# A list-scheduled two-layer diffusion backbone: new costs for TensorE and GpSimd in the planner, and a larger threshold for holding an instruction back

## The chip, the core and the metric

One core of a Trainium2 chip runs the whole program. The metric is device time in microseconds (us), the median of the runs. The engines are called by the profile's names: PE (TensorE matmul), PEld (TensorE weight load), DVE (VectorE), ACT (ScalarE), POOL (GpSimd) and SP (SyncE, which issues the DMAs). Each engine runs its own instructions strictly in the order in which the program holds them and waits on semaphores for the others.

## What is computed

Two layers of a backbone act on 256 latent tokens and 256 context tokens of width 1024, all in float32:

```
for each layer:                                   # mod: shift, scale, gate from silu(c) @ ada_w
    x, ctx = half_ffn(x), half_ffn(ctx)           # h + 0.5*gate*(silu(h w1) * (h w3)) w2, width 2816
    y_x, y_c = mixer(modulate(rms_norm(x)), modulate(rms_norm(ctx)))
    x, ctx = x + gate*y_x, ctx + gate*y_c
    x, ctx = half_ffn(x), half_ffn(ctx)           # the last layer has no context from the mixer on
```

The even layer's mixer has grouped-query attention beside latent attention, with normed queries and keys and a rotary step, on one input and one output projection. The odd layer's has a gated linear recursion in both directions (HGRN2) beside neighbourhood attention.

## The kernel before, in words

**Tiles.** Activations lie transposed, 128 features on the partitions by up to 512 tokens. A weight of 128 x 1024 is loaded by SP, its high part is rounded to float32r on ACT (`_prep`, line 527), and the low part, the difference, comes from DVE or POOL (`tt("vp", ...)`, line 484). A projection is then three products per chunk (high x high, low x high, high x low; `mm3`), summed in one PSUM bank of 512 columns. Small products, such as attention's scores of the latent kind, its values, transposes and the recursion's levels, stay in plain float32.

**Stages.** `ffn` (line 761) runs four times: ffn, `ab` (line 1131), ffn, ffn, `cd` (line 1317), ffn. The last one has the 256 latent tokens alone. In `group` (line 891) one weight group meets tokens in blocks of 128, each block in the next of a ring of PSUM banks; the evacuation of such a bank norms the heads: a square on ACT, a sum on DVE, a reciprocal square root (`rsqrt`, line 488) of fourteen small dependent instructions on POOL, a product on DVE, then transposes on PE. In the even mixer the ring has five banks (0, 1, 2, 3, 6) and serves five groups in turn. In the odd mixer `hgrn` runs for each half of the heads: eight levels, each with a memset of a key buffer on POOL, copies into it on ACT, small products on PE, a masked copy on DVE, two multiplications on DVE and, for the next level, a product on POOL (512, 256, ... 8 elements wide).

**The order of the instructions** is written by no one. Every call is recorded as an operation with its dependences (`record`, line 203), and `schedule` (line 268) plays them through with costs in ns (`cost`, line 163), fixed latencies between engines (`LAT`, times 1.2) and, on all engines but tensor and sync, a margin of 1.02 on the cost. Buffers and banks are rings in the order of recording, so an operation also waits for the users of the buffer that it takes over. At each step the engine that is free first takes the most urgent of the operations that are ready. An operation recorded for two engines goes to the one that gets to it first, unless the other would end it earlier. Urgency comes from `latest` (line 337), a backward pass; `justified` (line 388) plays ten rounds and keeps the one whose planned end is the earliest. `issue` emits the operations in the order of their planned starts.

One rule may leave an engine idle. If an operation that is more urgent by GAP becomes ready within WAIT ns, and the one at hand is longer than LONG, the engine waits for the urgent one:

```
soon = min((q for q in lh if q[0] < t + self.WAIT and q[1] < p - self.GAP and q[3].start is None), ...)
if soon is not None and var[4] > self.LONG:
    c = (soon[0], soon[1], e, soon[3], soon[4])
```

The change touches `LONG` (line 144) and `cost` (line 163).

Of the kernel before, what the change touches and what calls it, by code (L numbers as in the profile page):

```python
# [126 lines left out]
def is_bytes(dt):  # L127
    return 1 if dt == U8 else 4
# [6 lines left out]
class Program:  # L135
# [5 lines left out]
        "gpsimd": dict(tensor=230, vector=75, scalar=100, gpsimd=100, sync=100),  # L141
        "sync": dict(tensor=200, vector=200, scalar=200, gpsimd=200, sync=0),
    }
    WAIT, GAP, LONG = 500, 150, 250

    MARGIN = 1.02
    LAT = {a: {b: t * 1.2 for b, t in d.items()} for a, d in LAT.items()}
# [15 lines left out]
    def cost(self, eng, name, a, k, out, ins):  # L163
        n = out.size if isinstance(out, View) else 0
        if eng == "tensor":
            m = 128 if name == "transpose" else a[1].size
            if name == "transpose":
                return 109
            if a[1].buf.dtype == F32R:
                return max(n / 2.4 + 2.5, 26 + 0.64 * m)  # L170
            tiles = 128 // (out.p1 - out.p0) if m <= 64 else 1
            return max(4 * max(n, m) / 2.4 / tiles + 5 * tiles, 80)
        if eng == "sync" or name == "dma_start":
            v = out if isinstance(out, View) else ins[0]
            return max(60, (v.p1 - v.p0) * v.size * is_bytes(v.buf.dtype) / 360)
        m = max([n] + [v.size for v in ins])
        src_ps = any(v.buf.psum for v in ins)
        ptrs = sum(isinstance(v, View) and v.size == 1 for v in list(a[2:]) + [k.get("scalar1"), k.get("scalar2")])
        if eng == "scalar":
            more = (k.get("accum_out") is not None) + any(isinstance(k.get(x), View) for x in ("bias", "scale"))  # L180
            return 0.833 * m + (51 if src_ps else 93) + 93 * more
        if eng == "gpsimd":
            if name == "memset":
                return 36 + 0.83 * n
            return 148 + (2.1 if name == "tensor_tensor" else 3.6 if ptrs else 0.85) * m
        fast = name in ("tensor_scalar", "tensor_copy", "memset") and not src_ps and not (isinstance(out, View) and out.buf.psum)
        return 69 + m * (0.53 if fast else 1.04) + (60 * ptrs if name in ("tensor_scalar", "scalar_tensor_tensor") else 0)

# [1533 lines left out]
```

## Time and profile before

| | |
|---|---|
| median of 3 runs | 1829.24 us (1828.5 to 1829.32) |
| the profiled execution | 1828.99 us |
| its span, first to last instruction | 1827.2 us |
| mean granted TensorE clock | 0.993 |
| PE busy | 1785.3 us, 98% of the span |
| DVE, ACT, POOL busy | 69%, 41%, 12% |

A busy time is the time in which at least one instruction of an engine ran. PE's instructions overlap, and the ends of its matmuls are modelled, so a row's mean duration of a matmul is longer than the distance from one to the next. Every recorded operation is emitted by one helper, so all rows bear line 408 and are told apart by engine, operation, tile and shape. The tile `b` is a PSUM bank; `wh` and `wl` are a weight's parts; `rq_v`, `rq_w` and `rq_i` belong to the reciprocal square root; `gH` and `gL` are reused, in the odd mixer for the recursion's operands.

### The profile page before, as it was taken

How to read it: one execution, taken by the hardware profiler on the slowest of the kernel's cores; microseconds unless marked ns; L12 is line 12 of the kernel's file. 1: busy time of each engine (PE TensorE's matmuls, PEld its weight loads, DVE VectorE, ACT ScalarE, POOL GpSimd, SP SyncE). 2: the span in 40 equal slices, each digit the busy share in tenths (PEclk: the TensorE clock that was granted, in tenths of full speed). 3: DMA queues.
4: the chain of work that ended last, by engine and by line, in shares of the span. 5: the costliest groups of instructions: out<-in, count | busy, mean ns of one | idle time of the engine just before them, and what ended most of it. 6: DMA issues, size and time to landing. Idle time of an engine off the chain costs nothing.

```text
span 1827.2 us, 25949 instructions
## 1 busy us (share of the span) xinstructions
PE 1785.3 (98%) x9795; PEld 1496.0 (82%) x9795; DVE 1256.6 (69%) x2251; ACT 742.4 (41%) x1270; POOL 224.9 (12%) x537
## 2 busy tenths in 40 slices
PE   7999999999899999999999999999999999989999
PEld 5888888898686798888888988888888877788887
DVE  5587777768778786666766765445458777777775
ACT  5422322236566452222222522222226548756553
POOL 0100000003442011000000100000004102511111
PEclk9999999999899999999999999999999999999999
DMA  8364555513011145444443454444433322146563
GB/s 348 119 204 171 201 189 175 173 50 113 27 47 58 58 130 171 160 163 160 161 156 109 142 173 162 161 147 175 156 121 105 118 84 72 43 153 196 186 195 104
DMA packets 75692, 257.59 MB, mean 141 GB/s; under 512 B 9392, under 2 KB 13232, under 8 KB 74288
## 3 DMA queue, kind: packets, MB, share of 16 engines
q1 hardware_dynamic: 75568, 255.94, 42.4%
q8 instruction: 77, 1.26, 0.3%
q14 instruction: 47, 0.39, 0.1%
HBM read 254.86 MB, written 1.05 MB: 140 GB/s over the span
## 4 chain that ended last, share of the span: by engine, by line
PE 90%; DVE 4%; POOL 3%; ACT 2%; issue 1%; DMA 0%; DVEq 0%; ACTq 0%; POOLq 0%
PE b L408 90%; POOL rq_w L408 1%; DVE w L408 1%; DVE wl L408 1%; POOL rq_v L408 1%; ACT gL L408 1%; DVE m L408 0%; POOL rq_i L408 0%; DVE gH L408 0%; ACT w L408 0%; POOL gH L408 0%; DVE nacc L408 0%; DMA xX<-in_xT 0%; DVE p L408 0%; DVE ss L408 0%
## 5 line engine op out<-in xcount | busy, mean ns | idle before, releaser
L408 PE MATMUL b<-hH,wh 128*128 128x512 f32 (+1 forms) x1648 | 600.1, 382 | 3.4 <-DVE hH L408 2.9
L408 ACT CAST wh<-raw 128x1024 fp32r<-128x1024 f32 (+4 forms) x310 | 312.2, 1008 | 638.4 <-PE b L408 506.6
L408 PE MATMUL b<-hH,wl 128*128 128x512 f32 (+1 forms) x1616 | 560.6, 356 | 0.4 <-DVE wl L408 0.4
L408 DVE TENSOR_TENSOR wl<-raw,wh 128x1024 fp32r<-128x1024 f32 (+4 forms) x309 | 384.5, 1247 | 162.9 <-ACT wh L408 159.8
L408 PEld LDWEIGHTS b<-hH,wh 128*128 128x128 f32 x1648 | 307.2, 189 | 61.1 <-DVE hH L408 3.2
L408 PEld LDWEIGHTS b<-hH,wl 128*128 128x128 f32 x1616 | 305.1, 189 | 50.1 <-issue 2.5
L408 PE MATMUL b<-hL,wh 128*128 128x512 f32 (+1 forms) x1232 | 294.2, 374 | 0.0
L408 DVE SCALAR_TENSOR_TENSOR adas<-ada,m 128x1024 f32<-128x1024 f32 x224 | 273.4, 1221 | 26.5 <-DMA ada<-in_adaT 24.0
L408 PE MATMUL b<-gH,wh 128*128 128x512 f32 (+1 forms) x809 | 278.8, 366 | 0.0
L408 PE MATMUL b<-gH,wl 128*128 128x512 f32 (+1 forms) x809 | 263.9, 341 | 0.0
L408 PEld LDWEIGHTS b<-hL,wh 128*128 128x128 f32 x1232 | 219.4, 188 | 42.3 <-issue 1.6
L408 PEld LDWEIGHTS b<-gH,wh 128*128 128x128 f32 x809 | 150.7, 188 | 24.1
L408 PEld LDWEIGHTS b<-gH,wl 128*128 128x128 f32 x809 | 151.9, 188 | 21.5
L408 DVE SCALAR_TENSOR_TENSOR xX<-b,mod,xX 128x256 f32<-128x256 f32 x152 | 72.6, 482 | 100.3 <-PE b L408 98.6
L408 PE MATMUL b<-gL,wh 128*128 128x512 f32 (+1 forms) x633 | 135.2, 354 | 0.0
L408 PEld LDWEIGHTS b<-gL,wh 128*128 128x128 f32 x633 | 106.5, 188 | 17.5
L408 ACT ACTIVATE w<-b 128x512 f32<-128x512 f32 (+3 forms) x104 | 58.7, 566 | 152.5 <-PE b L408 152.3
L408 DVE TENSOR_TENSOR w<-w,b 128x512 f32<-128x512 f32 x66 | 45.4, 687 | 96.1 <-PE b L408 95.8
L408 PE MATMUL b<-wh,hH 128*128 128x512 f32 (+3 forms) x288 | 105.1, 368 | 2.9 <-ACT hH L408 1.7
L408 PE MATMUL b<-wl,hH 128*128 128x512 f32 (+3 forms) x288 | 105.0, 366 | 0.0
L408 PE MATMUL b<-wh,hL 128*128 128x512 f32 (+3 forms) x288 | 104.2, 364 | 0.0
L408 POOL TENSOR_TENSOR gL<-w,gH 128x512 fp32r<-128x512 f32 x22 | 31.5, 1432 | 584.4 <-ACT gH L408 584.4
(216 smaller groups left out, 1924.9 us busy)
## 6 DMA issues: line engine op xcount, KB each, us to landing
raw<-in_w SPq DMA_DIRECT2D x182, 512.0 KB, 3.5
ada<-in_adaT SPq DMA_DIRECT2D x128, 512.0 KB, 4.4
raw<-in_w SPq DMA_DIRECT2D x56, 448.0 KB, 3.4
ada<-in_w SPq DMA_DIRECT2D x22, 512.0 KB, 3.6
gH<-in_ada SPq DMA_DIRECT2D x4, 1024.0 KB, 10.2
raw<-in_ab_out SPq DMA_DIRECT2D x8, 512.0 KB, 3.7
raw<-in_cd_z SPq DMA_DIRECT2D x8, 512.0 KB, 3.6
ada<-in_w SPq DMA_DIRECT2D x8, 448.0 KB, 3.3
```

The lines of the kernel that those rows point to most:

```text
L408: getattr(getattr(nc, e), name)(*[fix(v) for v in a], **{n: fix(v) for n, v in k.items()})
```

## The change

`LONG` goes from 250 to 500. In `cost`, the formulas for PE, for POOL's instructions other than memset, and for DVE's scan are replaced. No instruction is added or removed and none gets other operands; the planner reckons anew, so the order on each engine, and the engine of the operations that have a choice, may differ. No other constant of the planner changes.

```diff
-    WAIT, GAP, LONG = 500, 150, 250
+    WAIT, GAP, LONG = 500, 150, 500
...
         if eng == "tensor":
-            m = 128 if name == "transpose" else a[1].size
             if name == "transpose":
-                return 109
+                return 110
             if a[1].buf.dtype == F32R:
-                return max(n / 2.4 + 2.5, 26 + 0.64 * m)
-            tiles = 128 // (out.p1 - out.p0) if m <= 64 else 1
-            return max(4 * max(n, m) / 2.4 / tiles + 5 * tiles, 80)
+                return max(n / 2.4 + 14, 110)
+            if a[1].size <= 64:
+                return max((0.98 if out.p1 - out.p0 == 64 else 0.6) * n, 79)
+            return max(4 * n / 2.4 + 10, 222)
...
         if eng == "gpsimd":
             if name == "memset":
                 return 36 + 0.83 * n
-            return 148 + (2.1 if name == "tensor_tensor" else 3.6 if ptrs else 0.85) * m
+            return (220 + 3.2 * min(m, 256) + 2.1 * max(m - 256, 0)) if name == "tensor_tensor" else 235 + (3.6 if ptrs else 0.9) * m
+        if name == "tensor_tensor_scan":
+            return 70 + 2.07 * m
         fast = name in ("tensor_scalar", "tensor_copy", "memset") and not src_ps and not (isinstance(out, View) and out.buf.psum)
         return 69 + m * (0.53 if fast else 1.04) + (60 * ptrs if name in ("tensor_scalar", "scalar_tensor_tensor") else 0)
```

Here `n` is the number of elements per partition that are written, `m` the largest such number among the operands, and `ptrs` the number of operands that are one column.

## Rows read from the trace of the kernel before

**Rows 1.** The page, part 1: busy us, share of the span, instructions.

```profile
PE 1785.3 (98%) x9795; PEld 1496.0 (82%) x9795; DVE 1256.6 (69%) x2251; ACT 742.4 (41%) x1270; POOL 224.9 (12%) x537
```

**Rows 2.** Windows by stage: length, PE, PEld, DVE, ACT, POOL busy, PEclk, DMA, GB/s.

```profile
25.30:407.00 381.70, 381.68 (x1880) 315.73 (x1881) 274.32 (x441) 114.79 (x167) 23.20 (x30) 1.00 0.51 169
407.00:645.00 238.00, 225.63 (x1332) 181.33 (x1330) 186.15 (x523) 141.59 (x345) 69.00 (x260) 0.98 0.19 60
645.00:1372.00 727.00, 726.98 (x3602) 615.14 (x3601) 449.38 (x689) 212.01 (x295) 34.28 (x28) 1.00 0.46 154
1372.00:1637.20 265.20, 251.66 (x1861) 212.09 (x1859) 203.68 (x367) 165.63 (x279) 71.17 (x193) 0.98 0.31 97
1637.20:1823.30 186.10, 185.98 (x1056) 162.32 (x1056) 128.69 (x188) 94.94 (x158) 27.00 (x22) 0.99 0.54 169
```

**Rows 3.** The same view in finer windows of the two mixers.

```profile
456.90:463.30 6.40, 0.22 (x1) 0.01 (x1) 3.76 (x6) 0.90 (x2) 5.92 (x31) 0.67 0.22 61
463.30:469.40 6.10, 6.08 (x19) 5.05 (x20) 4.58 (x7) 3.21 (x5) 4.04 (x20) 0.51 0.01 3
...
1575.30:1579.60 4.30, 0.27 (x4) 0.05 (x2) 0.64 (x2) 1.85 (x3) 3.11 (x3) 0.89 0.46 149
1579.60:1585.60 6.00, 6.00 (x50) 4.71 (x52) 4.82 (x9) 4.84 (x8) 0.95 (x1) 0.51 0.06 25
1585.60:1630.00 44.40, 44.23 (x468) 42.33 (x464) 33.24 (x55) 27.67 (x46) 11.84 (x33) 1.00 0.38 121
1630.00:1637.20 7.20, 2.18 (x12) 1.83 (x12) 6.68 (x20) 4.16 (x8) 0.00 (x0) 0.73 0.61 209
1637.20:1640.20 3.00, 2.98 (x10) 2.69 (x11) 3.00 (x8) 1.93 (x5) 0.74 (x1) 0.52 0.51 175
```

**Rows 4.** Timelines of PE, DVE and POOL around 457: start, us, instruction [idle before].

```profile
463.32 1.09 PE L408 MATMUL b<-ident,w 128*128 128x128 f32 x4 [6.20 <-DVE w L408]
...
454.05 0.69 DVE L408 TENSOR_REDUCE ss<-w 128x8 f32<-128x512 f32 x1
...
454.82 0.20 POOL L408 TENSOR_SCALAR rq_v<-ss 128x8 f32<-128x8 f32 x1 [5.13 <-DVE ss L408]
...
462.25 0.20 POOL L408 TENSOR_TENSOR ss<-rq_i,rq_w 128x8 f32<-128x8 f32 x1
```

**Rows 5.** Timelines from 1568 to 1580, POOL and PE.

```profile
1568.40 6.45 POOL L408 TENSOR_TENSOR gH<-gH 128x512 f32<-128x512 f32 x7
...
1574.82 1.82 POOL L408 TENSOR_TENSOR wl<-raw,wh 128x768 fp32r<-128x768 f32 x1
1576.58 1.84 POOL L408 MEMSET gL<- 128x1024 f32 x2
...
1579.58 1.71 PE L408 MATMUL b<-gL 128*64 128x32 f32 x28 [4.03 <-ACT gL L408]
```

**Rows 6.** One window of the first feed-forward block, columns as in rows 2.

```profile
100.00:200.00 100.00, 100.00 (x438) 81.82 (x437) 76.96 (x113) 24.63 (x29) 4.26 (x3) 1.00 0.56 188
```

**Rows 7.** Groups of POOL by shape: count | busy us, mean ns | idle before.

```profile
L408 POOL TENSOR_TENSOR gL<-w,gH 128x512 fp32r<-128x512 f32 x22 | 31.5, 1432 | 584.4 <-ACT gH L408 584.4
L408 POOL TENSOR_TENSOR gH<-w,gH 128x256 fp32r<-128x256 f32 x20 | 25.5, 1276 | 140.1 <-ACT gH L408 140.1
L408 POOL TENSOR_TENSOR hL<-w,hH 128x256 fp32r<-128x256 f32 x20 | 15.9, 796 | 162.3 <-ACT w L408 162.3
...
L408 POOL TENSOR_TENSOR rq_w<-rq_v,rq_i 128x8 f32<-128x8 f32 x42 | 10.1, 244 | 2.7
```

**Rows 8.** A group of DVE in the page's part 5.

```profile
L408 DVE SCALAR_TENSOR_TENSOR xX<-b,mod,xX 128x256 f32<-128x256 f32 x152 | 72.6, 482 | 100.3 <-PE b L408 98.6
```

**Rows 9.** Timelines of POOL and DVE at 1562.

```profile
1561.75 1.96 POOL L408 TENSOR_TENSOR rq_w<-rq_v,rq_i 128x4 f32<-128x4 f32 x1
...
1562.45 1.19 DVE L408 TENSOR_TENSOR wl<-raw,wh 128x1024 fp32r<-128x1024 f32 x1
```

## The prediction

> **What bounds the kernel now.** First the busy shares of the page [rows 1]: PE is busy 98% of the span, and no other engine comes over 69%. Then the busy time by stage [rows 2]. In the three stretches of feed-forward work PE is busy 381.68 of 381.70 us, 726.98 of 727.00 and 185.98 of 186.10: nothing that only reorders instructions can shorten them unless it removes PE work, and this change removes none. The reader is to see that all slack sits elsewhere: PE idles 238.00 - 225.63 = 12.4 us in the even layer's mixer (407 to 645) and 265.20 - 251.66 = 13.5 us in the odd layer's mixer (1372 to 1637.2). The first 25.3 us and the last 3.9 us hold the other idle time: loading and a last residual, whose costs the change does not touch.
>
> Then the same view, cut finer around the long waits [rows 3]. Three holes carry most of the mixers' idle time: 6.40 us with 0.22 us of PE work at 456.9, 4.30 us with 0.27 at 1575.3, and 7.20 us with 2.18 at 1630. After each of them the granted clock is about one half, that is 1.2 of 2.4 GHz, for 6.10, 6.00 and 3.00 us, though PE is then busy. At half clock half of that time is lost: 3.05, 3.0 and 1.5 us. So the three holes cost 6.2 + 3.05, 4.0 + 3.0 and 5.0 + 1.5 us. What is left of the mixers' 25.9 us of idle time is 25.9 - 15.2 = 10.7 us, in many short waits.
>
> Last the timeline at the two first holes. At 463.32 PE resumes with a transpose after 6.20 us of waiting for a product on DVE [rows 4]. That product waits for a reciprocal square root on POOL, which began at 454.82, right after DVE's reduction at 454.05, and whose last instruction starts at 462.25 [rows 4]: 7.4 us for fourteen small instructions, because other such chains share POOL. At 1579.58 PE starts a level of the HGRN recursion that waited for ScalarE, which waited for two memsets on POOL at 1576.58. In front of these POOL had seven products, 6.45 us from 1568.40, and a weight's low part of 1.82 us that could as well have run on DVE [rows 5].
>
> **PE's new costs.** One float32r product of 512 columns goes from 215.8 to 227.3 ns in the plan. In a full stretch the trace has 438 records in 100.00 us, 228 ns each [rows 6]: the new figure is right, the old one 5% short. PE does the same work at the same pace, so this is worth nothing directly. What it moves is the plan's idea of how far PE has got when a chain on POOL or DVE ends.
>
> **POOL's new costs.** With the margin of 1.02, a product or subtraction of 512 elements goes from 1247 to 1609 ns, of 256 from 700 to 1060, of 16 from 185 to 276, of 8 from 168 to 250. The trace's means are 1432 for the 512-wide subtraction, 1276 and 796 for two kinds of 256, 244 for 8 [rows 7]: nearer to the new figures than to the old, one of the 256-wide kinds excepted. For the hole at 1575 the seven products of one half (512, 256, 128, 64, 32, 16 and 8 wide) were planned at 1247 + 700 + 425 + 288 + 219 + 185 + 168 = 3.2 us. They took 6.45 us [rows 5]. The new plan gives them 1609 + 1060 + 643 + 434 + 329 + 276 + 250 = 4.6 us. So the old plan believed POOL free 3.2 us too early, and thought that the weight's low part fitted before the memset. The new plan is still 1.9 us short, but that low part of 768 now costs 2157 ns on POOL and stays at 885 on DVE, so it should go to DVE, or behind the memset. That frees the 1.82 us. Bounds for this hole: nothing, to the whole 4.0 us. I take 2.2, just over the one instruction that stands there by mistake, and 1.0 of the 3.0 us of slow clock, since the trace has the half clock behind the longest waits alone. A loss here is not excluded; it is priced below.
>
> For the hole at 457 the product waits for chains that the old plan put at 166 ns an instruction and the new one at 250. Fourteen in a row, each with the plan's 120 ns of latency, are 4.0 us by the old figures and 5.2 by the new; the trace has 7.4. The new plan is nearer and starts the chain's sources, the reduction on DVE among them, earlier in the order. But what could fill PE meanwhile is limited: the products of the next groups use the same five banks in turn, and these are held until the chains end. I take 2.2 us of the 6.2, the step from 5.2 to 7.4 being what the plan still doesn't see, and 1.5 of the 3.05 us of slow clock. Bounds: nothing, to 9.2 us together.
>
> **Which engine takes the optional work.** An instruction that may run on DVE or POOL is moved to POOL when DVE would end it later. For the 512-wide low part this needs a DVE delay of over 1247 - 613 = 634 ns before, over 1609 - 613 = 996 after. So POOL loses some of its 22 such subtractions [rows 7], and DVE gains at most 22 x 0.61 = 13.5 us. This hides under PE: DVE is busy 274.32 of 381.70 us in the first feed-forward stretch and less than that share in the second [rows 2]. If that cover went, it would be those 13.5 us at most. I take nothing.
>
> **The scan** on DVE is planned at 612 instead of 342 ns: sixteen instructions, no work changed; nothing.
>
> **Holding back.** LONG goes from 250 to 500 ns. Instructions planned between the two no longer leave the engine idle for a more urgent one that comes within 500 ns. The residual of 256 columns is one, planned at 403 ns and 482 in the trace [rows 8]. Such an instruction can now delay an urgent one by its own length, while the engine loses less idle time. Bounds: a gain inside the 10.7 us of short waits, or a loss that the rivals price. Of the short waits I take 1.0 us off for plan and threshold together, with 4 us either way, since a new order moves these waits as easily as it ends them. The hole at 1630 is the last norm before a feed-forward block: nothing else is left for PE there, so it stays.
>
> **Sum.** 2.2 + 1.0 + 2.2 + 1.5 + 1.0 = 7.9 us. The profiled execution took 1828.99 us (span 1827.2), 0.25 us under the median of 1829.24, so one sum serves both: 1829.0 - 7.9 = 1821.1 us, call it 1821.
>
> **Rivals.** *No change: POOL's time is set by its neighbour.* At 1561.75 one 4-wide product on POOL takes 1.96 us, where an 8-wide one takes 0.20 [rows 4], and DVE's two-operand subtraction that starts at 1562.45 and takes 1.19 us ends at 1563.64, as the POOL instruction ends [rows 9]. If the long POOL times come from what DVE happens to run beside them, a fixed cost places no wait better, and the holes only move: about 1829, within 3.6 us. Beside it stands the Trainium skill, page "SBUF — State Buffer", section "Who interferes with whom": a VectorE instruction with two SBUF inputs contends with a GpSimd instruction that reads SBUF, and the later one waits for the whole of the other. By that rule no constant describes POOL; the trace agrees at this one place. For the rival also speaks that five shared banks limit what can fill the first hole; against it, that the mean of a group already has such waits in it. Chance 0.23.
>
> *Slower: short work in front of the odd layer's chain.* In the second half of the recursion the chain runs from POOL over ScalarE to PE and DVE and back, eight times, while the out-projection's eight residuals and as many squares for the norm run on DVE and ScalarE. All of these are short in the plan, so none is held back any more. If each stands in front of a chain instruction for the 0.482 us of a residual [rows 8], the chain ends 16 x 0.482 = 7.7 us later, and PE has nothing else once the out-projection is through: 1829 + 7.7 = 1836.7. It decides if these delays exceed what the two holes give back, that is from about 8 of the 16 on, if the holes give half of their 6.9 us. For it: the old threshold kept exactly these apart. Against it: between 1585.6 and 1630 PE is busy 44.23 of 44.40 us [rows 3], so some delay is covered. Chance 0.21.
>
> *Full gain.* Both holes close and the clock stays up: 9.2 + 7.0 us, and 1 of short waits: 1829 - 17 = 1812. Chance 0.08.
>
> *The change doesn't do what it says*: PE's and POOL's costs are means only of some kinds (796 against 1276 for one width [rows 7]), so the plan may be no truer than before. Its time is that of the first rival, and its chance is within that one's.
>
> **How the numbers follow.** The forecast, 1814 to 1825, has 0.48; with the full gain, faster is 0.56. A change under 0.2% of 1829, some 3.7 us, is about what a measurement of this kernel cannot tell from none: 0.23, and slower 0.21. The range goes from 1810, within the full gain, to 1835, within the slower case; what it leaves out is a few hundredths below and about 0.14 above. The likeliest case's own range is 1814 to 1825.
>
> **What would show it.** In the changed kernel: the feed-forward stretches as long as before within a microsecond; fewer than 22 of the 512-wide subtractions on POOL; no weight's low part on POOL in front of a memset in the recursion; PE's wait for the first rsqrt chains shorter than 6.2 us; less time at half clock. The forecast is wrong if the mixers' two stretches together are not shorter than 503.2 us (238.0 + 265.2), if new holes of several microseconds stand elsewhere in them, or if DVE now holds PE up in the feed-forward work.

## The result, and the profile after

| | before | after |
|---|---|---|
| median of 4 runs each, us | 1829.28 (1828.5 to 1830.81) | 1842.56 (1838.09 to 1844.42) |
| ratio, with its 95% interval | | 1.0069 [1.0056, 1.0082] |
| profiled execution, us | 1828.99 | 1838.09 |
| its span; mean granted clock | 1827.2; 0.993 | 1836.3; 0.996 |

The change makes the kernel 13.3 us slower. The forecast was 8 us faster, 1821 us; 1842.56 lies above its range of 1810 to 1835. The execution that was profiled is the fastest of the four.

The page of the kernel after, part 1 (busy us, share, instructions), answers to [rows 1]:

```profile
PE 1799.2 (98%) x9795; PEld 1494.0 (81%) x9795; DVE 1257.4 (68%) x2300; ACT 744.7 (41%) x1276; POOL 152.3 (8%) x482
```

PE runs the same 9795 instructions, has a higher mean clock, and is busy 13.9 us longer than before. The reader is to see that first: PE's work is the same, and it needs more time for it.

Windows of the kernel after, columns as in [rows 2]: the first and the second feed-forward stretch, one window within the first (as [rows 6]), the first long wait of the even mixer with what follows it and a second wait, the place of the hole at 1575, and the last norm.

```profile
21.90:411.30 389.40, 389.38 (x1894) 317.76 (x1895) 274.30 (x455) 115.83 (x169) 10.35 (x20) 1.00 0.50 170
654.56:1381.40 726.84, 726.63 (x3519) 605.16 (x3520) 438.01 (x683) 202.41 (x277) 7.71 (x8) 1.00 0.45 152
...
100.00:200.00 100.00, 100.00 (x431) 80.73 (x430) 76.25 (x116) 24.12 (x28) 0.00 (x0) 1.00 0.53 182
...
461.50:466.05 4.55, 0.39 (x3) 0.04 (x1) 3.05 (x5) 0.00 (x1) 4.22 (x22) 0.96 0.25 81
466.00:470.00 4.00, 3.88 (x14) 3.07 (x14) 2.15 (x4) 2.32 (x4) 2.58 (x16) 0.61 0.05 21
480.90:484.07 3.17, 0.41 (x3) 0.01 (x1) 1.84 (x6) 2.65 (x4) 2.59 (x14) 1.00 0.00 0
1575.00:1620.00 45.00, 42.06 (x479) 36.85 (x478) 35.25 (x52) 37.13 (x62) 12.40 (x23) 1.00 0.31 98
1639.00:1644.30 5.30, 1.51 (x7) 1.16 (x7) 3.65 (x18) 1.18 (x3) 0.00 (x0) 0.58 0.57 189
1644.30:1649.50 5.20, 5.18 (x17) 4.50 (x18) 4.57 (x11) 4.29 (x9) 1.47 (x2) 0.50 0.00 0
```

In the mixers the planner did much of what was hoped. The first hole is down from 6.40 to 4.55 us, and behind it stand 4.00 us at a clock of 0.61 where 6.10 us at 0.51 stood before [rows 3]; a hole of 3.17 us follows at 480.9, with the clock at 1.00. Around 1575 the clock is 1.00 throughout. But in the window from 100 to 200, where PE is busy all the time at full clock in both kernels, 438 records [rows 6] have become 431. The windows of whole stretches do not hold the same products before and after (3602 records in 727.00 us [rows 2], 3519 in 726.84), so their lengths do not compare; the same products are followed further down.

What PE waited for, in total, times, longest (us). The three lines of the kernel before:

```profile
PE b L408 <- DVE w L408: 9.2, 5, 6.2
PE b L408 <- ACT gL L408: 4.6, 2, 4.0
...
PE b L408 <- ACT p L408: 0.8, 1, 0.8
```

and of the kernel after:

```profile
PE b L411 <- DVE w L411: 4.9, 3, 4.2
PE b L411 <- ACT p L411: 2.8, 1, 2.8
PE b L411 <- DVE nrs L411: 2.4, 2, 2.1
...
PE b L411 <- ACT gL L411: 1.9, 4, 0.6
```

The two forecast waits shrank, 6.2 to 4.2 us and 4.0 to 0.6; the new one at 481 is the 2.8 us for a softmax tile `p`. So the 13.3 us are not in PE's waits. They are in the distance from one product to the next. The timeline of PE, four successive records before (start, us, instruction):

```profile
221.15 0.39 PE L408 MATMUL b<-hH,wh 128*128 128x512 f32 x1
221.38 0.39 PE L408 MATMUL b<-hH,wl 128*128 128x512 f32 x1
221.60 0.39 PE L408 MATMUL b<-hH,wh 128*128 128x512 f32 x1
221.83 0.39 PE L408 MATMUL b<-hH,wl 128*128 128x512 f32 x1
```

and after:

```profile
219.75 0.40 PE L411 MATMUL b<-hH,wl 128*128 128x512 f32 x1
219.99 0.40 PE L411 MATMUL b<-hH,wh 128*128 128x512 f32 x1
220.22 0.40 PE L411 MATMUL b<-hH,wl 128*128 128x512 f32 x1
220.46 0.40 PE L411 MATMUL b<-hH,wh 128*128 128x512 f32 x1
```

The same two products in turn: 0.68 us for three steps before, 0.71 after. It is the same instruction on tiles of the same shape at the same granted clock. What differs is where the tiles lie. A tile gets its address at its first use in the issued order (`make`, called by `issue`), so a new order gives new addresses. In the compiled programs (each tile's start in bytes within its partition) one 32-byte slot (`nrs`, buffer 1) lies in front of `mod0`, `gL` and `hH` before and behind them after, so that `gL` and `hH` start 32 bytes lower, at 320 instead of 352 bytes past a multiple of 512; `hL` and ten of the twelve weight buffers start at 352 in both. `gH` starts at 0 in both.

### The profile page after: what moved, and what is told of

Read it like the earlier page. It is cut to its first block, busy times and chain, and to the rows that moved or that the text cites. A ratio compares the mean times of both kernels' runs of the same rounds, so it can differ in the third digit from the quotient of the medians.

```text
span 1836.3 us, 25848 instructions
## 1 busy us (share of the span) xinstructions
PE 1799.2 (98%) x9795; PEld 1494.0 (81%) x9795; DVE 1257.4 (68%) x2300; ACT 744.7 (41%) x1276; POOL 152.3 (8%) x482
## 4 chain that ended last, share of the span: by engine, by line
PE 90%; DVE 4%; ACT 4%; issue 1%; POOL 1%; DMA 0%; ACTq 0%; DVEq 0%
PE b L411 90%; ACT gL L411 2%; DVE w L411 1%; DVE wl L411 1%; ACT wh L411 1%; DVE hL L411 0%; ACT w L411 0%; DVE gH L411 0%; DVE m L411 0%; DMA xX<-in_xT 0%; POOL rq_w L411 0%; ACT L411 0%; ACT gH L411 0%; DVE nacc L411 0%; ACT m L411 0%
## 5 line engine op out<-in xcount | busy, mean ns | idle before, releaser
L411 DVE TENSOR_TENSOR wl<-raw,wh 128x1024 fp32r<-128x1024 f32 (+4 forms) x310 | 363.7, 1174 | 227.3 <-ACT wh L411 223.5
L411 POOL TENSOR_TENSOR nacc<-nacc,w 128x256 f32<-128x256 f32 x5 | 7.3, 1457 | 735.4 <-ACT w L411 731.4
```

The source lines that it names most:

```text
L411: getattr(getattr(nc, e), name)(*[fix(v) for v in a], **{n: fix(v) for n, v in k.items()})
```

## The experiments

**Theory (places):** PE's pace depends on where the moving tile and the weights lie, and the new addresses cost the time. **Rival (order):** the new order itself slows PE, by what runs beside it. To tell them apart, a kernel's first buffers are made in a fixed order, whatever the instructions' order is. This edit is in every experiment; they differ in the list `LAYOUT`, and in whose planner they have:

```diff
     def issue(self, nc):
         end, order = self.justified()
+        sb = self.rings["ones"][0].pool
+        for tag, n in LAYOUT:
+            if tag == "pad":
+                sb.tile([128, 8], F32, tag=f"pad_{n}", name=f"pad_{n}")
+            else:
+                self.rings[tag][n].make()
```

A pad takes 32 bytes. Each kernel ran beside the kernel before on the same chip, and its ratio is against that.

**1. The changed planner with the old places.** The list has the first uses of the kernel before.

```diff
+    ("nrs", 0), ("pt", 0), ("vA", 0), ("nrs", 1), ("mod0", 0), ("gL", 0), ("hH", 0), ("hL", 0),
```

> The changed kernel's order of instructions, but every tile and bank at the address that it has in the kernel before. Places theory (the new order hands out other addresses, since a tile gets its place at its first use, and the distance between PE's products depends on them): the window from 100 to 200 us has about 438 products again instead of 431, the first feed-forward stretch is back from 389 to about 382 us, and the time falls by 12 to 22 us below the changed kernel's, to between 1820 and 1830. Order theory (the instructions that now run beside PE slow it): 431 products stay, and the time stays within 4 us of the changed kernel's.

Measured: 1826.26 us (11 runs) against 1828.88, ratio 0.9987 [0.9979, 0.9996]. The change's order, without its addresses, is 2.6 us faster than before. The stretch named in the expectation did not come back to 382 us: by windows set in the same way it is 387.90, with 1897 records. Those bounds take in other work than before; over the same products the sign holds, as the table behind experiment 12 shows (288.0 us from the first to the second column, 287.8 before, 292.0 after).

**2. The old planner with the new places.** The list has the first uses of the kernel after.

```diff
+    ("vA", 0), ("pt", 0), ("mod0", 0), ("gL", 0), ("hH", 0), ("nrs", 1), ("hL", 0),
```

> The kernel before in its own order, with every tile and bank at the address that it has in the changed kernel. Places theory: about 431 products in the window from 100 to 200 us, and 1840 to 1850 us in all. Order theory: 438 products and 1829 us, as before.

Measured: 1844.44 us (5 runs), ratio 1.0085 [1.0072, 1.0099]. The addresses alone cost 15.6 us. The window from 100 to 200 in experiment 1:

```profile
100.00:200.00 100.00, 100.00 (x437) 81.86 (x436) 76.57 (x116) 24.17 (x28) 0.00 (x0) 1.00 0.54 186
```

and in experiment 2:

```profile
100.00:200.00 100.00, 100.00 (x431) 80.74 (x430) 76.20 (x110) 24.72 (x29) 4.26 (x3) 1.00 0.56 185
```

The pace follows the places (437 and 431), not the order: the rival falls. DVE's and POOL's load in experiment 2 (76.20, 4.26) is near that of the kernel before (76.96, 4.26 [rows 6]), so what runs beside PE is not the cause either. Since the kernel after and experiment 1 have the same order, their 9795 records pair one to one. The kernel after gains 3.9 us of lag on experiment 1 from 100 to 390, nothing (0.1) from 390 to 645, 9.0 from 645 to 1372, and 1.3 from there to 1740: it loses where large products stand back to back.

**3. All tiles 32 bytes higher.** The old planner and places, with one pad in front.

```diff
-    ("ones", 0), ("xX", 0), ("pt", 2),
+    ("pad", 0), ("ones", 0), ("xX", 0), ("pt", 2),
```

> The kernel before with one unused piece of 32 bytes in front of all tiles: every tile moves by 32 bytes, and the distances between tiles stay. Absolute form of the places theory (a moving operand that starts at an odd multiple of 32 bytes streams at about 227 ns a product of 512 columns, one at a multiple of 64 at about 233): hH, hL and gL change to 64, gH to odd, so the distances swap, 431 to 433 products in the window, and 1838 to 1845 us. Relative form (what counts is whether weight and moving operand lie alike): nothing changes, 438 products, 1829 us. Order theory: nothing changes.

Measured: 1828.71 us (10 runs), ratio 0.9998 [0.9989, 1.0007]. No absolute address matters; only places relative to each other do.

**4. `gH` moved by 32 bytes, all behind it by 64.** A first form of the theory held that moving tile and weights must agree modulo 64.

```diff
-    ("gH", 0), ("nacc", 1),
+    ("pad", 0), ("gH", 0), ("pad", 1), ("nacc", 1),
```

> The kernel before with gH, alone of the four moving operands at a multiple of 64 bytes, moved to an odd multiple of 32; all other tiles keep their address modulo 64. Both forms of the places theory: products with gH go from about 233 to 227 ns; there are some 1000 of 512 columns, so 5 to 7 us less than before, 1822 to 1824 us. Order theory: 1829 us, no change.

Measured: 1828.55 us (10 runs), ratio 0.9995 [0.9986, 1.0004]. A miss. `gH` now starts at 32 past a multiple of 512 and the weights at 416: they agree modulo 64 and 128 but not modulo 256 or 512, and the products of `gH` are no faster on the whole. The next form was modulo 512.

**5 and 6. All weights and activations at the same place modulo 512.** `gH` moves behind `hL`, and the two odd weight buffers behind the other ten; all start at 352. Experiment 5 has the old planner, 6 the changed one.

```diff
-    ("gH", 0), ("nacc", 1), ("adab1", 0), ("rq_v", 0), ("rq_i", 0), ("wh", 0), ("rq_w", 0), ("wl", 0),
+    ("nacc", 1), ("adab1", 0), ("rq_v", 0), ("rq_i", 0), ("rq_w", 0),
...
-    ("hL", 0), ("wh", 1),
+    ("hL", 0), ("gH", 0), ("wh", 1),
...
-    ("wh", 5), ("wl", 5), ("ada", 0),
+    ("wh", 5), ("wl", 5), ("wh", 0), ("wl", 0), ("ada", 0),
```

> The kernel before in its own order, with gH, wh's first and wl's first buffer laid among the other large tiles, so that all moving operands and all weight buffers of the feed-forward blocks start at 352 modulo 512. Places theory in the form that the trace now suggests (a product is fast when its moving operand and the weight loaded beside it start at the same address modulo 512): some 1000 products with gH and a sixth of the others lose 5 to 6 ns, 8 to 12 us in all: 1817 to 1821 us, 440 records in the window. If gH's slowness has another cause: 1825 to 1829 us.

> The changed kernel's order with the same places as the run before this one. If order and place add up: the 2.6 us that the changed order gave with the old places, on top of the run before: 1814 to 1819 us, and below both kernels. If they don't: as the run before this one or slower.

Measured: 1821.19 us (5 runs), ratio 0.996 [0.9948, 0.9972], and 1817.69 us (6 runs), ratio 0.9939 [0.9927, 0.9951]. The same window in experiment 5:

```profile
100.00:200.00 100.00, 100.00 (x443) 82.81 (x442) 78.17 (x114) 25.63 (x30) 4.28 (x3) 1.00 0.58 194
```

and in experiment 6:

```profile
100.00:200.00 100.00, 100.00 (x443) 82.81 (x442) 78.74 (x120) 24.54 (x29) 0.00 (x0) 1.00 0.56 191
```

443 records, whichever the order. Experiment 6 is faster than both kernels of this case: it has the change's order, and all large tiles in phase.

**7. One tile moved.** The changed planner with its own places, but `nrs` 1 back in front of `mod0`. PSUM banks stay where the change puts them.

```diff
-    ("mod0", 0), ("gL", 0), ("hH", 0), ("nrs", 1), ("hL", 0),
+    ("nrs", 1), ("mod0", 0), ("gL", 0), ("hH", 0), ("hL", 0),
```

> The changed kernel with its own order and its own places, but for one tile: the second 8-byte buffer of the norm's reciprocal root is laid in front of the conditioning table instead of behind hH, so hH and gL lie 32 bytes higher, at the same address modulo 512 (352) as hL and ten of the twelve weight buffers. Places theory: products with hH and gL go from about 233 to 227 or 228 ns, 437 records in the window from 100 to 200 us, 1824 to 1830 us. Order theory: 1842 us as for the changed kernel.

Measured: 1826.4 us (12 runs), ratio 0.9991 [0.9981, 1.0]. One slot of 32 bytes is worth 1842.56 - 1826.4 = 16.2 us. The banks are not the cause.

**8. `hH` alone out of phase.** The old planner and places, one pad in front of `hH` and fifteen behind it, so that all that follows keeps its place modulo 512.

```diff
-    ("gL", 0), ("hH", 0), ("hL", 0),
+    ("gL", 0), ("pad", 0), ("hH", 0), ("pad", 1),
...
+    ("pad", 15), ("hL", 0),
```

> The kernel before with hH alone laid 32 bytes higher, out of phase with the weight buffers; all other tiles keep their address modulo 512. Phase form of the places theory: products with hH go from about 228 to 232 or 234 ns, those with hL and gL stay at 227, and with some 2500 products of 512 columns on hH the time is 10 to 16 us longer: 1839 to 1845 us. If the absolute address counted or the operands together: hL and gL change too, or nothing does.

Measured: 1845.11 us (4 runs), ratio 1.0084 [1.0071, 1.0098], with 432 records in the window:

```profile
100.00:200.00 100.00, 100.00 (x432) 80.86 (x432) 76.22 (x110) 24.51 (x29) 4.27 (x3) 1.00 0.57 187
```

Here is the mean distance in ns from the start of a 512-column product to the next record, from 100 to 400 us, by weight and moving tile, worked out from PE's records:

```
                 wh,hH   wl,hH   wh,hL   wh,gH   wl,gH   wh,gL
before           227.7   228.5   227.2   233.2   234.4   227.1
after            232.0   233.7   230.0   233.6   233.9   233.3
1 old places     227.7   228.5   227.2   233.3   234.4   227.9
2 new places     232.0   233.7   230.0   233.6   233.9   233.3
4 gH moved       227.7   228.5   227.2   236.1   229.6   229.0
5 in phase       226.7   226.7   226.6   226.7   226.7   226.6
7 one tile       227.9   227.4   227.8   233.7   233.8   228.5
8 hH out         232.9   234.2   230.9   233.3   234.4   227.0
```

Lines 1 and 2 stand on the lines of before and after, although the orders are exchanged. In line 8 the products of `hH` are slow, as expected, and those of `gL` are not (227.0). But those of `hL`, which is in phase, were expected to stay at 227 and went to 230.9: they are slower for a while behind products of `hH` out of phase. PE's records show how long. In a run of eight products of `hL` with weights at 352, the mean distances in experiment 8 are 240.8, 224.2, 230.8, 235.8, 228.4, 232.5, 230.7 and 226.8 ns, so it is over at the eighth; before, all eight are between 226.5 and 226.7. Not every mix does this: `gL` behind the out-of-phase `gH` stays between 226 and 228 in both.

The line of before also holds the effect within one kernel. PE's records and the program's products come in the same order, so each product's buffer is known: `hH` with `wh` takes 226.7 ns with the five buffers at 352 (208 products) and 232.4 with the one at 96 (48), with `wl` 226.7 with the five at 352 (208) and 236.5 with the one at 128 (48).

The modulus 512 fits all lines. 64 and 128 are excluded by experiment 4. Larger powers of two are excluded by experiment 5: the weights' chunks lie 512 bytes apart, so the places differ there by 0 or 512 modulo 1024, and both kinds are at 227 (612 and 580 products). 256 was not told apart: the products 256 apart in the kernel before all stand among or behind products with `wl` at 128.

**9 to 12. The parts of the change, all with the old places.** In 9 only LONG has its new value; in 10 all costs are new and LONG is 250; in 11 only PE's costs are new; in 12 only POOL's and the scan's.

```diff
-    WAIT, GAP, LONG = 500, 150, 250
+    WAIT, GAP, LONG = 500, 150, 500
```

is the edit of 9, and the other three take their part of the change's `cost` with LONG at 250.

> The kernel before with the larger threshold for holding back alone (500 in place of 250), old costs, old places. If the threshold brought the order's small gain: 1825 to 1827 us. If it costs time, as the rival of short work in front of the chain had it: 1831 to 1837 us. If it does nothing by itself: 1829 us.

> All new costs without the larger threshold, old places. The forecast's view (the truer costs bring the gain of the order): 1824 to 1827 us, like the whole change with old places. If the threshold is needed beside them (small POOL instructions are planned at 250 ns, just at the old threshold): 1828 to 1833 us.

> PE's new costs alone, old threshold, old places. The forecast gave them nothing by themselves: 1827 to 1831 us. If the pace of PE in the plan carries the gain: 1823 to 1826 us.

> POOL's and the scan's new costs alone, old threshold, old places. The forecast laid the whole gain on them: 1823 to 1827 us, the wait at the recursion's second half and the weight's low part in front of the memset gone. If they are no truer than the old ones: 1828 to 1833 us.

Measured, medians of 10 or 11 runs each:

| | us | ratio |
|---|---|---|
| 9, LONG alone | 1827.92 | 0.9994 [0.9986, 1.0003] |
| 10, all costs, not LONG | 1828.26 | 0.9994 [0.9986, 1.0003] |
| 11, PE's costs alone | 1834.25 | 1.0026 [1.0017, 1.0035] |
| 12, POOL's and the scan's costs alone | 1829.2 | 0.9995 [0.9986, 1.0004] |
| 1, all of it | 1826.26 | 0.9987 [0.9979, 0.9996] |

No part alone gains anything measurable, and PE's costs alone lose 5 us, though they are the truer figures. By the expectations, 10 came out as if the threshold were needed beside the costs, 11 lies outside both of its ranges, and 9 comes nearest to a threshold that does nothing by itself, and 12 has the time of costs that are no truer, although the wait that it named did go. The interval of all of it overlaps those of 9, 10 and 12, so the gain of 2.6 us is not divided among the parts. Where each order stands is seen by following products that every kernel has: the table gives by how many us the n-th product of a tile with `wh` starts later (+) or earlier (-) than in the profile of before, worked out from one profiled execution each.

```
product of before at us       103.8   391.6   660.3  1361.1  1690.5
                             hL 97  gH 191  hL 386  gH 585  gH 654
after                         -0.2    +4.0    +1.9   +11.7    +8.6
1 changed, old places         +1.9    +2.1    +0.2    +0.9    -3.3
9 LONG alone                  -0.4    -0.8    -3.4    -3.4    -2.1
10 all costs, not LONG        -1.5    -1.3    -1.0    -0.4    -2.6
11 PE's costs                 -1.0    -0.8    -1.7    -0.6    +4.7
12 POOL's costs               -1.3    -1.3    +2.3    +2.3    -1.8
```

From the second column to the third lies the even mixer, from the fourth to the fifth the odd one. In experiment 1 the even mixer gains 1.9 us and the odd one 4.2. POOL's costs alone gain 4.1 in the odd one and lose 3.6 in the even one; PE's costs alone lose 5.3 in the odd one. The lines of PE's waits in experiment 11 show where (total, times, longest):

```profile
PE b L415 <- DVE w L415: 11.7, 9, 2.8
...
PE b L415 <- ACT gL L415: 5.5, 6, 1.6
PE b L415 <- DVE nrs L415: 5.2, 2, 4.4
```

The recursion's waits for `gL` are back at 5.5 us (1.9 after), and the longest wait for a norm's `nrs` is 4.4, where it is 2.1 after.

## Why the prediction was wrong

**The step that failed** is the first one: that in the three feed-forward stretches nothing that only reorders instructions can shorten them unless it removes PE work, and that PE "does the same work at the same pace". I read a share of 100% as a fixed duration. The busy time holds the distance between products, and that distance moved from 227.7 to 232.0 ns for `wh,hH`, because a reordering here also moves tiles. Worth: 16.3 us between the medians of the kernel after and experiment 1, 15.6 in experiment 2 with the old order. Over the same products the changed kernel takes 4.2 us more from 103.8 to 391.6 and 9.8 more from 660.3 to 1361.1; experiment 1, with the same order, takes 0.2 and 0.8 more. Neither the sum nor any rival had such a term, so the sign came out wrong. The diff could have raised the question: addresses follow first use in the issued order, and the change makes a new order.

The view that I used for it said so as well, had it been read by pair of tiles: in the kernel before, the products of `gH` stood 233 to 234 ns apart and those of `hH` 228, at the same shape and clock. The 228 ns that I took from 438 records [rows 6] was a mean over products of two kinds.

Here the Trainium skill, page "Perfetto Trace Analysis", section "Identifying the Most-Contended Engine", warns that the matmul busy share is not a good measure of how close a kernel is to roofline, because pipelined PE instructions look smaller in the trace. On the share the traces agree: PE's is 98% in the kernel before and in the kernel after, with 13.3 us between their medians.

**The hole at 457** was to give 2.2 us and 1.5 of slow clock. The wait shrank by 2.0 (6.2 to 4.2), and of the slow clock behind it 4.00 x (1 - 0.61) = 1.6 us are left of 3.05: both terms had about the right size. But the wait for `p` grew by 2.0 (0.8 to 2.8). By the products' starts the even mixer gains 1.9 us in experiment 1, half of the 3.7. The term that was missed is the next late thing: the step named only the banks as what limits this. The cause was wrong too. The step laid this gain on POOL's costs, and with these alone (experiment 12) the wait stays at 5.84 us; the threshold alone (9) brings it to 3.43, PE's costs alone (11) to 2.75 with another of 1.98 in front of it. The lines of PE in experiments 12, 9 and 11, in this order:

```profile
464.17 1.09 PE L416 MATMUL b<-ident,w 128*128 128x128 f32 x4 [5.84 <-DVE w L416]
461.00 0.63 PE L414 MATMUL b<-ident,w 128*128 128x128 f32 x4 [3.43 <-DVE w L414]
461.95 0.63 PE L415 MATMUL b<-ident,w 128*128 128x128 f32 x4 [2.75 <-DVE w L415]
```

So that the term had the right size is luck; how the threshold and PE's costs shorten this wait was not followed.

**The hole at 1575** was to give 2.2 and 1.0 of slow clock. The mechanism held. The timeline of POOL after (start, us, instruction, idle before) answers to [rows 5]:

```profile
1576.62 3.31 POOL L411 TENSOR_TENSOR gH<-gH 128x512 f32<-128x512 f32 x6 [3.89 <-DVE gH L411]
1581.39 0.96 POOL L411 MEMSET gL<- 128x1024 f32 x1 [1.47 <-PE b L411]
1582.31 1.26 POOL L411 TENSOR_TENSOR gH<-gH 128x8 f32<-128x8 f32 x1
```

No weight's low part stands in front of the memset any more, and the memset waits for PE, not PE for it. The odd mixer gains 4.2 us in experiment 1, more than the 3.2 of the sum. Here POOL's costs are shown to be the cause: alone, in experiment 12, they take PE's longest wait for `gL` from 4.0 us to 0.6, and its odd mixer gains 4.1.

```profile
PE b L416 <- ACT gL L416: 1.8, 4, 0.6
```

**Short waits** were to give 1.0, with 4 us either way; the parts of the change moved a mixer by anything from 5.3 us later (PE's costs, the odd one) to 2.6 earlier (LONG, the even one), the 4.1 of POOL's costs in the odd one aside. With the mixers at 1.9 + 4.2 = 6.1 the sum of 7.9 was of the right size for what it spoke of. But experiment 1 is only 2.6 us faster by the medians, a third of the sum, so the order by itself would not have borne the forecast out either. In its profile, 1.9 us are lost before 103.8 and 0.8 between 660.3 and 1361.1. The first stretch starts later in some executions of this order and not in others (the kernel after is 0.2 early at the same product), and the medians' spread is wider (1824.01 to 1828.72 in experiment 1). Experiment 2, with the old order, is 1.9 us late at the same product in its profile too, so the late start does not need the new order; what causes it was not settled. The sentence that the change does not touch the opening's costs was argued from the instructions and not from their order.

**Costs that were taken at nothing.** The optional work moved off POOL, as forecast. Groups of POOL after, which answer to [rows 7] (count | busy us, mean ns | idle before):

```profile
L411 POOL TENSOR_TENSOR hL<-w,hH 128x256 fp32r<-128x256 f32 x20 | 17.2, 862 | 477.4 <-DVE w L411 343.9 <-ACT w L411 95.7 <-issue 37.8
...
L411 POOL TENSOR_TENSOR gH<-gH 128x8 f32<-128x8 f32 x2 | 2.4, 1210 | 0.1
...
L411 POOL TENSOR_TENSOR gH<-gH 128x512 f32<-128x512 f32 x2 | 2.2, 1097 | 3.9 <-DVE gH L411 3.9
```

The group of DVE's low parts, before:

```profile
L408 DVE TENSOR_TENSOR wl<-raw,wh 128x1024 fp32r<-128x1024 f32 (+4 forms) x309 | 384.5, 1247 | 162.9 <-ACT wh L408 159.8
```

and after:

```profile
L411 DVE TENSOR_TENSOR wl<-raw,wh 128x1024 fp32r<-128x1024 f32 (+4 forms) x310 | 363.7, 1174 | 227.3 <-ACT wh L411 223.5
```

All 22 of the 512-wide subtractions are gone from POOL, and the weight's low part with them: DVE has 310 of those where it had 309. DVE's busy time grew by 0.8 us, not by 13.5, since its low parts took 20.8 us less (384.5 to 363.7), with less on POOL beside them; that this is the cause fits [rows 9] but was not tried by itself. The cover named for DVE's work was there.

**The rivals.** *No change* falls as a result, but with the old places (experiment 1) the time would lie in its band of 3.6 us around 1829. Its mechanism is in the rows: the plan puts 1609 ns on a 512-wide product that takes 1097 here and 250 on an 8-wide one that takes 1210, and POOL's costs alone gave nothing in all (experiment 12). What runs beside POOL was not varied by itself. The place that the rival pointed at agrees in its end alone: POOL's product starts 0.70 us ahead of DVE's subtraction [rows 9], so by these records it is the earlier one that takes longer. *Slower, by short work in front of the odd chain,* has the right sign and the wrong cause: LONG alone gives 1827.92 us, and its odd mixer loses 1.3 us, not 7.7. *Full gain* falls.

**The signs named ahead.** The feed-forward stretches as long as before within a microsecond: wrong, by the 4.2 and 9.8 us above, and this was the sign that told. Fewer than 22 subtractions, no low part in front of the memset, a first wait under 6.2 us: right. Less half clock: right in the mean (0.993 to 0.996). At the last norm PE idles less, 5.30 - 1.51 = 3.8 us against 7.20 - 2.18 = 5.0, and yet 5.20 us at a clock of 0.50 follow, against 3.00 at 0.52 [rows 3]. Of the signs that it is wrong, the mixers told nothing: over the same products they are 2.1 and 3.1 us shorter in the kernel after, and one new hole, of 3.17 us, stands in the even one.

## What to carry to other kernels

Reordering instructions can move tiles in memory, and moving a tile can change the pace of a full engine. So compare the distance between equal instructions before comparing waits, group it by tile and not only by shape, and when a scheduling change is measured, hold the addresses fixed and judge the order by itself. Here fixed addresses turned a loss of 13.3 us into a gain of 2.6, and addresses that agree, with the same order, into one of 11.3 (1829.0 to 1817.69). A truer cost in one place of a planner need not help: PE's costs alone lost 5 us.

## What the runs showed of the hardware that was not expected

The distance between float32r products of 512 columns depends on whether the moving tile and the weights start at the same place modulo 512 bytes: 226.7 ns where they do (experiment 5, all pairs), 229.6 to 236.1 where they don't (`gH` before, after and in experiment 4), and up to 230.9 for products in phase that follow others out of phase. The modulus could as well be 256, as far as the runs show. The effect is relative (experiment 3), and 32 bytes are enough (experiments 7 and 8). Why it is so, the runs don't show. The Trainium skill, page "SBUF — State Buffer", section "Who interferes with whom", gives PE two independent read ports, for the moving operand and for the weight load, and says that PE never waits on anyone. Read as a rule for PE's own two reads, it would put all pairs at one pace; the table has 226.7 and 234.4 ns for the same product at different places, so the measurement decides against that reading here.
